# Attention's queries and keys stored in two token orders instead of read with a step

## The chip, the cores and the metric

The kernel runs on one core of a Trainium2 chip. The metric is the device time of one execution in microseconds, as the median of several runs. TensorE multiplies matrices; VectorE, ScalarE and GpSimd work on elements; SyncE issues nearly all transfers, which sixteen DMA engines carry out.

## The reference

One encoder layer runs on 2048 prompt tokens and on 256 sample tokens (2304 in the kernel): RMSNorm and a combined projection; beside each other dilated windowed attention (8 heads of 64) and a bidirectional gated delta rule; then an output projection and a gated feed-forward block. The part that counts here is attention's scores:

```python
DILATED_PATTERNS = ((128, 1), (512, 4), (2048, 16))
...
    def to_sub(t):
        return t.reshape(b, ld, dilation, h, dh).transpose(0, 2, 1, 3, 4).reshape(b * dilation, ld, h, dh)

    num, m, den = _band_attention(to_sub(q), to_sub(k), to_sub(v), window // (2 * dilation))
...
    for part in parts[1:]:
        sc = jnp.exp(part[1] - m_all)
        num = num + part[0] * sc[..., None]
        den = den + part[2] * sc
    return num / den[..., None]
```

Each token attends to 64 neighbours on either side, three times: among all tokens, among those with its residue mod 4, and among those with its residue mod 16. The three results are merged by their denominators. Queries and keys are normalised per head and rotated first.

## The kernel before, in words

**Production** (`att_tile`, line 1341). The normalised input lies in HBM as 9 windows of 256 tokens. A window is loaded (line 240), and for each of its two tiles of 128 tokens and each of two column blocks b (line 1362) TensorE projects queries and keys (`toks`, line 251), VectorE and GpSimd normalise and rotate them, four transposes (line 1393) bring them to channels x tokens, and the result is split into a rounded high part qh (line 1395) and a rest ql (line 1397). Both go to HBM in natural token order (line 1399), in runs of 128 tokens. There are three passes: three windows with both blocks (from line 1417), six windows with block 0 (line 1424), the same six with block 1 (line 1442). The delta rule's scan (`scan`, line 858) takes its steps in between, loading and storing its own operands, and the maxima of head 0 (`first_head`, line 1405) are made in the third pass.

**Attention** (`steady`, line 1227). Heads run one behind the other, 21 groups a head: one for the sample, four of dilation 16, eight pairs of dilation 4, eight of dilation 1. A group has a score step s, an exponential step e (ScalarE, then masks on GpSimd, line 1035) and a value step v. TensorE's order is written out by hand: at step g it issues the scores of group g + 2, some pieces of the next heads' row maxima (line 971, reduced on VectorE at line 974), and the values of group g. Score and maximum products read tokens of one residue as every fourth or sixteenth element of the natural order (`pview`, line 958), both as the weights loaded and as the moving operand:

```python
            nc.tensor.matmul(out, lhsT=kv, rhs=qv, start=True, stop=False)
            nc.tensor.matmul(out, lhsT=k1v, rhs=qlv, start=False, stop=True)
```

The first product contracts over 128 rows: k's high and low parts against q's high part, which VectorE writes twice (`twice_q`, line 945). The second contracts over 65: k's high part with a row of ones (copied by `twice_k`, line 955) against q's low part with a row of negated maxima.

**Loads of a head.** `load_qk` (line 936) and `load_ql` (line 949) bring four tiles of 64 rows x 2304 tokens; q and k have three buffers, the other two tiles two. `load_values` (line 920) brings the values three times, once for each dilation's order, in runs of 64 elements. The maxima go through HBM: `max_store` (line 1008) stores them and loads them back in another order, `max_row` (line 1024) combines them on VectorE, stores the row and loads it into row 64 of ql (line 1032). The denominators take a like way (lines 1189 to 1209). All of this is issued by SyncE into one queue; SyncE's own order is set by a planner from when operands should be ready, while the order on the other four engines in attention is the program's.

## Time and profile before

| | us |
|---|---|
| median of 3 runs (lowest to highest) | 3485.42 (3480.18 to 3487.45) |
| the profiled execution's own time | 3489.7 |
| its span, first to last instruction | 3488.0 |
| TensorE busy | 3300.0 (95%) |
| VectorE busy | 2284.4 (65%) |
| ScalarE busy | 1626.4 (47%) |
| GpSimd busy | 1739.3 (50%) |
| DMA queue of SyncE, share of 16 engines | 46.0% |

Times in the rows count from the span's start. A row of the timeline begins with the start and the duration of what it names; matrix products are pipelined, so the time one product costs is read from start to start, not from its duration. "65*128 65x256" is a product of 65 rows, 128 weight columns and 256 moving columns. "x4" says that four in a row were merged.

### The profile page before, as it was taken

The page shows a single profiled execution, that of the slowest core. Times are in us where ns is not written, and L with a number is a line of the kernel's source. Part 1 is how long each engine was busy: PE and PEld are TensorE (multiplying, and loading weights), DVE is VectorE, ACT ScalarE, POOL GpSimd, SP SyncE. Part 2 cuts the span into 40 slices and gives each one's busy share as a digit, 9 for nine tenths or more (in the row PEclk, how much of TensorE's full clock was granted, in tenths as well). Part 3 has the DMA queues.
Part 4 walks back from the last instruction along what each step waited for, and adds up shares of the span by engine and source line. Part 5 has one row for each costly group of instructions (what it writes and reads, how often), then busy time and mean ns, then how long its engine had stood idle before and what let it go on. Part 6 is the DMA issues. An engine that isn't in the chain of part 4 may idle for free.

```text
span 3488.0 us, 57839 instructions
## 1 busy us (share of the span) xinstructions
PE 3300.0 (95%) x20191; PEld 3005.9 (86%) x20191; DVE 2284.4 (65%) x6044; ACT 1626.4 (47%) x3404; POOL 1739.3 (50%) x1736
## 2 busy tenths in 40 slices
PE   7899899999999979999889899999999999999999
PEld 6888788887987869999677899998899998899998
DVE  7899775675899966675565455557555556555555
ACT  5665534334443346667232444445544445544443
POOL 4323521111345334444122766776866777866774
PEclk9999899999999969999999999999999999999999
DMA  5555555458997865541776422223422222422221
GB/s 186 195 203 202 183 182 171 158 168 280 313 313 217 276 141 111 118 101 46 170 180 150 145 67 66 65 69 97 142 70 61 67 70 79 163 61 67 70 73 49
DMA packets 494313, 483.78 MB, mean 139 GB/s; under 512 B 131303, under 2 KB 405346, under 8 KB 488253
## 3 DMA queue, kind: packets, MB, share of 16 engines
q1 hardware_dynamic: 492357, 474.87, 46.0%
q10 hardware_dynamic: 1296, 4.72, 0.4%
q8 instruction: 160, 2.62, 0.3%
q14 instruction: 132, 1.08, 0.1%
q0 software_dynamic: 368, 0.49, 0.1%
HBM read 337.77 MB, written 142.14 MB: 138 GB/s over the span
## 4 chain that ended last, share of the span: by engine, by line
PE 69%; DVE 17%; DMA 7%; issue 3%; ACT 2%; SPq 1%; POOL 0%; DVEq 0%; ACTq 0%; POOLq 0%
PE psy L1798 5%; PE psy L1799 5%; PE psy L1800 5%; PE psx L1607 4%; PE psx L1606 4%; PE psx L1605 4%; PE pvo L1162 3%; PE psv L1607 3%; PE psv L1605 3%; PE psv L1606 3%; PE pam L971 2%; PE pss L1052 2%; PE pss L1053 2%; PE psh L1322 1%; PE psy L1607 1%
## 5 line engine op out<-in xcount | busy, mean ns | idle before, releaser
L204 POOL TENSOR_TENSOR wring<-ws,wring 128x512 fp32r<-128x512 f32 x260 | 340.1, 1313 | 286.1 <-ACT wring L203 273.0
L1801 DVE TENSOR_TENSOR ya<-ya,psy 128x512 f32<-128x512 f32 x396 | 269.5, 685 | 218.9 <-PE psy L1800 217.4
L1798 PE MATMUL psy<-dh,hh 128*128 128x512 f32 x792 | 311.5, 395 | 7.6 <-ACT hh L1758 6.0
L1799 PE MATMUL psy<-dl,hh 128*128 128x512 f32 x792 | 312.6, 395 | 0.0
L1800 PE MATMUL psy<-dh,hl 128*128 128x512 f32 x792 | 307.5, 396 | 1.5 <-DVE hl L1759 1.5
L203 ACT CAST wring<-ws 128x512 fp32r<-128x512 f32 x260 | 161.3, 620 | 287.1 <-PE psv L1606 143.3
L204 POOL TENSOR_TENSOR wring<-raw,wring 128x512 fp32r<-128x512 f32 x195 | 254.1, 1305 | 72.1 <-ACT wring L203 68.5
L247 PE MATMUL psc<-nt,whi 128*128 128x260 f32 x864 | 255.3, 295 | 27.2 <-DVE kqt L269 5.6
L1035 POOL TENSOR_SCALAR_AFFINE_SELECT pt<-pt 128x256 f32<-128x256 f32 (+3 forms) x400 | 164.7, 435 | 231.1 <-ACT pt L1049 124.9
L249 PE MATMUL psc<-nt,wlo 128*128 128x260 f32 x864 | 251.2, 291 | 0.0
L248 PE MATMUL psc<-nt,whi 128*128 128x260 f32 x864 | 250.6, 290 | 0.0
L203 ACT CAST wring<-raw 128x512 fp32r<-128x512 f32 x195 | 121.0, 621 | 180.9 <-PE psx L1606 93.8
L974 DVE CUSTOM_DVE_ANT_0 mj<-pam,misc 128x256 f32<-128x256 f32 (+2 forms) x400 | 146.6, 367 | 81.0 <-PE pam L971 69.4
L247 PEld LDWEIGHTS psc<-nt,whi 128*128 128x128 f32 x864 | 168.2, 195 | 33.3 <-ACT kqt L261 8.2
L204 POOL TENSOR_TENSOR dl<-raw,dh 128x512 fp32r<-128x512 f32 x132 | 167.5, 1301 | 48.5 <-ACT dh L203 48.5
L1556 POOL TENSOR_TENSOR ws<-raw 128x512 f32<-128x512 f32 x130 | 169.0, 1300 | 24.4 <-DVE hn2l L1514 10.4
L1800 PEld LDWEIGHTS psy<-dh,hl 128*128 128x128 f32 x792 | 148.9, 188 | 35.2 <-DVE hl L1759 2.6
L1798 PEld LDWEIGHTS psy<-dh,hh 128*128 128x128 f32 x792 | 149.0, 188 | 31.2 <-ACT hh L1758 7.3
L249 PEld LDWEIGHTS psc<-nt,wlo 128*128 128x128 f32 x864 | 168.5, 195 | 0.7
L248 PEld LDWEIGHTS psc<-nt,whi 128*128 128x128 f32 x864 | 168.3, 195 | 0.7
L1378 POOL TENSOR_TENSOR r<-xn,ct 128x512 f32<-128x512 f32 x36 | 52.3, 1453 | 229.9 <-DVE xn L1371 189.6
L1799 PEld LDWEIGHTS psy<-dl,hh 128*128 128x128 f32 x792 | 149.2, 188 | 19.0
(435 smaller groups left out, 10615.2 us busy)
## 6 DMA issues: line engine op xcount, KB each, us to landing
raw<-in_w_up SPq DMA_DIRECT2D x260, 256.0 KB
nt<-nt_d SPq DMA_DIRECT2D x20, 2080.0 KB
raw<-in_w_down SPq DMA_DIRECT2D x132, 256.0 KB
nt_d<-nt SPq DMA_DIRECT2D x9, 2080.0 KB
xt<-in_x_prompt SPq DMA_DIRECT2D x24, 512.0 KB
raw<-in_w_in SPq DMA_DIRECT2D x20, 512.0 KB
kq_d<-kqt SPq DMA_DIRECT2D x18, 512.0 KB
kq<-kq_d SPq DMA_DIRECT2D x18, 512.0 KB
```

The costliest lines, as they stand in the source:

```text
L203: nc.scalar.copy(hi, raw)
L204: (sub or nc.gpsimd).tensor_tensor(out=lo, in0=raw, in1=f32(hi), op=ALU.subtract)
L247: nc.tensor.matmul(ps[:, 0:n], lhsT=hi, rhs=f32r(nt[:, 0, k, c0 : c0 + n]), start=k == 0, stop=False)
L248: nc.tensor.matmul(ps[:, 0:n], lhsT=hi, rhs=f32r(nt[:, 1, k, c0 : c0 + n]), start=False, stop=False)
L249: nc.tensor.matmul(ps[:, 0:n], lhsT=lo, rhs=f32r(nt[:, 0, k, c0 : c0 + n]), start=False, stop=k == KT - 1)
L1605: nc.tensor.matmul(ps[:, 0:m], lhsT=hi[:, k], rhs=bh[:, k, 0:m], start=start and k == 0, stop=False, skip_group_check=not start)
L1606: nc.tensor.matmul(ps[:, 0:m], lhsT=hi[:, k], rhs=bl[:, k, 0:m], start=False, stop=False, skip_group_check=not start)
L1607: nc.tensor.matmul(ps[:, 0:m], lhsT=lo[:, k], rhs=bh[:, k, 0:m], start=False, stop=stop and k == KH - 1, skip_group_check=not start)
L1798: nc.tensor.matmul(ps, lhsT=hh, rhs=dh[:, ns], start=gi == 0, stop=False)
L1799: nc.tensor.matmul(ps, lhsT=hh, rhs=dl[:, ns], start=False, stop=False)
L1800: nc.tensor.matmul(ps, lhsT=hl, rhs=dh[:, ns], start=False, stop=gi == len(group) - 1)
L1801: nc.vector.tensor_tensor(out=ya[:, i, ns], in0=ya[:, i, ns], in1=ps, op=ALU.add)
```

## The change

Production also stores queries and keys of the prompt by residue mod 4 (`qr_d`): ScalarE copies each part into an order of four residues, two tiles are gathered, and a window is stored in runs of 64 elements. In the first pass a window's two tiles now run inside the loop over blocks. In attention the first product contracts over 65 rows, high parts with the rows of maxima and ones, in tiles held twice (`firsts`, one set for each parity of the head, each in both orders); the second over 128 rows, k's low part against q's high part and k's high against q's low, in tiles held once and cut into four halves (`seconds`). Dilation 4 now reads contiguous columns, dilation 16 every fourth. The maxima use 64 rows of `firsts`. The order of groups and of the loads in `steady` changes with it.

```diff
     qk_d = [dram.tile([2, 4, P, T], F32, name=f"qk{b}_d") for b in range(2)]
+    qr_d = [dram.tile([2, P, 4, 4, SEQ // 4], F32, name=f"qr{b}_d") for b in range(2)]
...
     sh_d = dram.tile([AH, T], F32, name="sh_d")
+    one_d = dram.tile([1, T], F32, name="one_d")
+    sr_d = dram.tile([AH, SEQ], F32, name="sr_d")
...
-    aorder = [4, 0, 7, 1, 6, 2, 5, 3, 8]
+    aorder = [4, 0, 7, 8, 1, 6, 2, 5, 3]
...
         nc.sync.dma_start(dst[:, 32:48], src[0:SEQ].rearrange("(p r) d -> p r d", r=16))
         yield
         for r in range(4):
             nc.sync.dma_start(
                 dst[:, 16 + 4 * r : 20 + 4 * r], src[0:SEQ].rearrange("(t p r) d -> r p t d", p=P, r=4)[r]
             )
+        yield
         nc.sync.dma_start(dst[:, 0:16], src[0:SEQ].rearrange("(t p) d -> p t d", p=P))
+        nc.sync.dma_start(dst[:, 48:50], src[SEQ:T].rearrange("(t p) d -> p t d", p=P))
...
-    def load_qk(h):
+    HALVES = ((0, 0, 1024), (0, 1024, 2048), (1, 0, 1088), (1, 960, T))
+    def source(h, order, part, key):
         (b, j), rows = divmod(h // 2, 2), head_rows(h)[1]
-        qq, kk = qqs[h % 3], kks[h % 3]
-        nc.sync.dma_start(qq[0:DH], qk_d[b][0, j, rows])
-        nc.sync.dma_start(kk[0:DH], qk_d[b][0, 2 + j, rows])
-        nc.sync.dma_start(kk[DH:P], qk_d[b][1, 2 + j, rows])
-        heads[h].update(qq=qq, kk=kk)
-    def twice_q(h, copy=nc.vector.tensor_copy):
-        qq = heads[h]["qq"]
-        copy(f32r(qq[DH:P]), qq[0:DH])
-    def load_ql(h):
-        (b, j), rows = divmod(h // 2, 2), head_rows(h)[1]
-        heads[h].update(ql=qls[h % 2], k1=k1s[h % 2])
-        return nc.sync.dma_start(qls[h % 2][0:DH], qk_d[b][1, j, rows])
-    def twice_k(h):
-        nc.vector.tensor_copy(f32r(heads[h]["k1"][0:DH]), heads[h]["kk"][0:DH])
-    def pview(ap, dil):
-        return ap[:, 0:SEQ].rearrange("p (n r) -> p r n", r=dil)
+        if order == 0:
+            return qr_d[b][part, rows, 2 * key + j].rearrange("p r m -> p (r m)")
+        return qk_d[b][part, 2 * key + j, rows]
+    def load_first(h, order):
+        n = (SEQ, T)[order]
+        for key in range(2):
+            nc.sync.dma_start(firsts[h % 2][order][key][0:DH, 0:n], source(h, order, 0, key))
+    def load_second(h, half):
+        order, lo, hi = HALVES[half]
+        for key in range(2):
+            for i in range(2):
+                nc.sync.dma_start(seconds[half][key][DH * i : DH * i + DH], source(h, order, i ^ key, key)[:, lo:hi])
+    def load_row(h):
+        nc.sync.dma_start(firsts[h % 2][1][0][DH : DH + 1, 0:T], sh_d[h : h + 1, :])
+        heads[h]["row"] = nc.sync.dma_start(firsts[h % 2][0][0][DH : DH + 1, 0:SEQ], sr_d[h : h + 1, :])
+    def set_ones(h):
+        for order, n in enumerate((SEQ, T)):
+            nc.sync.dma_start(firsts[h % 2][order][1][DH : DH + 1, 0:n], one_d[:, 0:n])
+    def cols(dil, r, lo, hi):
+        if dil == 1:
+            return slice(lo, hi)
+        if dil == 4:
+            return slice(512 * r + lo, 512 * r + hi)
+        return slice(512 * (r % 4) + r // 4 + 4 * lo, 512 * (r % 4) + r // 4 + 4 * (hi - 1) + 1, 4)
...
-        hd = heads[h]
-        q, k = f32r(hd["qq"]), f32r(hd["kk"])
-        mx = hd["mx"] = pe.tile([P, 52], F32, name="mx", bufs=2)
+        mx = heads[h]["mx"] = pe.tile([P, 52], F32, name="mx", bufs=2)
+        q1, k1 = [[f32r(firsts[h % 2][o][key][0:DH]) for o in range(2)] for key in range(2)]
...
+        for r in range(4):
+            piece(
+                [(P * j, P, q1[0][:, cols(16, r + 4 * j, 0, P)], k1[0][:, cols(16, r + 4 * j, 0, P)], band[:, 256:384], 32 + r + 4 * j) for j in range(4)]
+            )
             yield
-        piece([(256 * t, 256, q[:, SEQ + P * t : SEQ + P * t + P], k[:, SEQ:T], scnt[:, t, :], 48 + t) for t in range(2)])
+            for t0 in (0, 2):
+                banded(4, r, t0)
+                yield
+        for t0 in range(0, 16, 2):
+            banded(1, 0, t0)
+            yield
+        piece([(256 * t, 256, q1[1][:, SEQ + P * t : SEQ + P * t + P], k1[1][:, SEQ:T], scnt[:, t, :], 48 + t) for t in range(2)])
         yield
...
-        sh = pe.tile([P, 16], F32R, name="sh", bufs=2)
+        sh = pe.tile([P, 16], F32R, name="sh", bufs=1)
         nc.vector.tensor_scalar(out=sh, in0=mm[:, 0], scalar1=-1.0, scalar2=None, op0=ALU.mult)
+        sr = pe.tile([P, 4, 4], F32R, name="sr", bufs=1)
+        nc.vector.tensor_scalar(
+            out=sr, in0=mm[:, 0].rearrange("p (j r) -> p r j", r=4), scalar1=-1.0, scalar2=None, op0=ALU.mult
+        )
         nc.sync.dma_start(sh_d[h, 0:SEQ].rearrange("(p n) -> p n", n=16), f32(sh))
-        heads[h]["row"] = nc.sync.dma_start(heads[h]["ql"][DH : DH + 1, :], sh_d[h : h + 1, :])
+        nc.sync.dma_start(sr_d[h].rearrange("(r p j) -> p r j", r=4, j=4), f32(sr))
+        load_row(h)
...
-        def score(out, kv, k1v, qv, qlv):
-            nc.tensor.matmul(out, lhsT=kv, rhs=qv, start=True, stop=False)
-            nc.tensor.matmul(out, lhsT=k1v, rhs=qlv, start=False, stop=True)
+        def score(out, half, keys, queries):
+            order, at, _ = HALVES[half]
+            q1, k1 = [f32r(firsts[h % 2][order][key][0 : DH + 1]) for key in range(2)]
+            q2, k2 = [f32r(seconds[half][key]) for key in range(2)]
+            moved = lambda c: slice(c.start - at, c.stop - at, c.step)
+            nc.tensor.matmul(out, lhsT=k1[:, keys], rhs=q1[:, queries], start=True, stop=False)
+            nc.tensor.matmul(out, lhsT=k2[:, moved(keys)], rhs=q2[:, moved(queries)], start=False, stop=True)
...
         def single(r0):
             st = {}
-            kv, k1v, qv, qlv = [pview(x, 16) for x in (kk, k1, qq, ql)]
             def s():
                 ps = st["ps"] = bank("mm", "pss")
                 for u in range(4):
-                    r = r0 + u
-                    score(ps[:, P * u : P * u + P], kv[:, r, :], k1v[:, r, :], qv[:, r, :], qlv[:, r, :])
+                    c = cols(16, r0 + 4 * u, 0, P)
+                    score(ps[:, P * u : P * u + P], r0 // 2, c, c)
...
-                    ks = slice(P * t, P * t + P)
-                    score(ps[:, o : o + hi - lo], kv[:, r, ks], k1v[:, r, ks], qv[:, r, lo:hi], qlv[:, r, lo:hi])
+                    half = 2 + t // 8 if dil == 1 else r // 2
+                    score(ps[:, o : o + hi - lo], half, cols(dil, r, P * t, P * t + P), cols(dil, r, lo, hi))
...
-        out += [single(r0) for r0 in range(0, 16, 4)]
         for r in range(4):
             pts, ob = {}, {}
-            out += [pair(4, 16, r, t0, pts, ob) for t0 in (0, 2)]
+            out += [single(r)] + [pair(4, 16, r, t0, pts, ob) for t0 in (0, 2)]
         pts, ob = {}, {}
         out += [pair(1, 0, 0, t0, pts, ob) for t0 in range(0, 16, 2)]
-        out.insert(0, sample())
+        out.insert(16, sample())
         return out
...
-        direct = {3: (SEQ, T), 15: (0, 448), 17: (448, 960), 19: (960, 1472), 20: (1472, SEQ)}
+        NP1 = 7
+        direct = {14: (0, 448), 16: (448, 960), 17: (SEQ, T), 19: (960, 1472), 20: (1472, SEQ)}
...
-                if (h, g) == (0, 1):
-                    twice_q(1)
-                if (h, g) == (0, GK):
-                    nc.vector.tensor_copy(f32r(k1s[1][DH : DH + 1]), ones[DH : DH + 1, 0:1].to_broadcast([1, T]))
-                if g == 0 and h + 1 < AH:
-                    with tc.issue_after(heads[h]["row"].ins):
-                        ql_in = load_ql(h + 1)
-                    with tc.issue_after((heads[h]["row"] if h else ql_in).ins):
-                        if h + 2 < AH:
-                            load_qk(h + 2)
+                if g == 11 and h + 1 < AH:
+                    with tc.issue_after(tail):
                         for _ in load_values(h + 1):
                             pass
...
                     s, e, _v = todo[n + LAG]
                     s()
                     e()
+                if g == 9 and h + 2 < AH:
+                    load_first(h + 2, 0)
+                if g == 18 and h + 2 < AH:
+                    load_first(h + 2, 1)
+                if g in (3, 9, 13, 18) and h + 1 < AH:
+                    load_second(h + 1, (3, 9, 13, 18).index(g))
                 if h + 1 < AH:
-                    for _ in range(((2 if h == 1 else 1) if g < G1 else 0) if h else (R0 if g >= G0 else 0)):
+                    if (h, g) == (0, 0):
+                        pieces[1] = max_pieces(1)
+                    for _ in range(0 if g > NP1 else 3 if h == 0 and g >= 1 else 2 if g in (3, 5) else g >= 1):
                         next(pieces[h + 1], None)
-                    if g == 1:
-                        twice_k(h + 1)
-                if h + 2 < AH:
-                    g1 = G1 if h else G3
-                    if g == g1 - 2:
-                        twice_q(h + 2)
-                    if g == g1:
+                if h + 2 < AH and g >= NG - 8:
+                    if g == NG - 8:
                         pieces[h + 2] = max_pieces(h + 2)
-                    if g >= g1:
-                        next(pieces[h + 2], None)
+                    for _ in range(1 + g % 2):
+                        next(pieces[h + 2])
                 todo[n][2]()
                 n += 1
                 if h + 1 < AH:
-                    if g == (G1 if h else G2):
+                    if g == NP1:
                         for _ in pieces[h + 1]:
                             pass
                         max_store(h + 1)
-                    if g == (G1 if h else G2) + 4:
+                    if g == NP1 + 4:
                         max_row(h + 1)
                 if h > 0:
                     if g == 4:
                         den_inv(h - 1)
                         den_rows(h - 1, 0)
-                    if g in (9, 13):
-                        den_mul(h - 1, (g - 9) // 4)
-                    if g == 9:
+                    if g in (10, 17 if h < AH - 1 else 13):
+                        den_mul(h - 1, int(g > 10))
+                    if g == 10:
                         den_rows(h - 1, 1)
                 if h == AH - 1 and g in (2, 6, 10, 14):
-                    load_wo(4 + g // 4, staged(pd), *wo[4 + g // 4])
+                    load_wo(4 + g // 4, pd.tile([P, D], F32, name="raw", bufs=1), *wo[4 + g // 4])
...
-        def att_tile(t, nt, c0, blocks):
+        byres = {}
+        def att_tile(t, nt, c0, blocks, last=False):
...
-                rr = rsqrt(pb, ss, [P, AH], 1.0 / DH, EPS, "na")
+                rr = rsqrt(pb, ss, [P, AH], 1.0 / DH, EPS, "na", bufs=1)
...
-                qh = pb.tile([P, 4, P], F32R, name="qh", bufs=2)
+                free = (p3, ("sk", "sq") if t % 2 else ("stk", "su"), 2) if last else (pb, ("qh", "ql"), 1)
+                qh, ql = [free[0].tile([P, 4, P], F32R, name=x, bufs=free[2]) for x in free[1]]
                 nc.scalar.copy(qh, pt.rearrange("p (j t) -> p j t", j=4))
-                ql = pb.tile([P, 4, P], F32R, name="ql", bufs=2)
                 nc.vector.tensor_tensor(out=ql, in0=pt.rearrange("p (j t) -> p j t", j=4), in1=f32(qh), op=ALU.subtract)
                 for i, part in enumerate((qh, ql)):
                     nc.sync.dma_start(
                         qk_d[b][i, :, :, t * P : (t + 1) * P].rearrange("j p t -> p j t"), f32(part)
                     )
+                    if t >= NTP:
+                        continue
+                    if t % 2 == 0:
+                        byres[b, i] = pb.tile([P, 4, 4, 64], F32, name=f"qr{i}", bufs=1)
+                    nc.scalar.copy(
+                        byres[b, i][:, :, :, 32 * (t % 2) : 32 * (t % 2) + 32], f32(part).rearrange("p j (m r) -> p j r m", r=4)
+                    )
+                    if t % 2 == 1:
+                        m0 = 64 * (t // 2)
+                        nc.sync.dma_start(qr_d[b][i, :, :, :, m0 : m0 + 64], byres[b, i])
...
         def first_head():
-            load_qk(0)
-            load_ql(0)
-            nc.scalar.copy(f32r(k1s[0][DH : DH + 1]), ones[DH : DH + 1, 0:1].to_broadcast([1, T]))
-            twice_q(0)
-            twice_k(0)
+            for order in range(2):
+                load_first(0, order)
+            set_ones(0)
...
-            for i in range(2):
+            for b in range(2):
                 with tc.high_priority():
                     scan()
-                att_tile(2 * w + i, nt, 2 + P * i, (0, 1))
+                for i in range(2):
+                    att_tile(2 * w + i, nt, 2 + P * i, (b,))
...
-                for _ in range(FH):
-                    next(fh, None)
-                att_tile(2 * w + i, nts[w], 2 + P * i, (1,))
+                with tc.high_priority():
+                    for _ in range(FH):
+                        next(fh, None)
+                att_tile(2 * w + i, nts[w], 2 + P * i, (1,), wi == NB - 1)
                 scan()
...
+        def second(pool, i):
+            _, lo, hi = HALVES[i]
+            return [pool.tile([P, hi - lo], F32, name=f"{x}2{i}") for x in "qk"]
+        seconds = [second(pa, 0)]
+        load_second(0, 0)
...
+        firsts.append([[pa.tile([DH + 1, n], F32, name=f"{x}1{o}") for x in "qk"] for o, n in enumerate((SEQ, T))])
+        sctx.close()
         pk = kctx.enter_context(pool("at3k"))
-        qqs.append(pk.tile([P, T], F32, name="qq2"))
-        kks.append(pk.tile([P, T], F32, name="kk2"))
-        qls.append(pk.tile([DH + 1, T], F32, name="ql1"))
-        k1s.append(pk.tile([DH + 1, T], F32, name="k1_1"))
-        pieces = {1: max_pieces(1)}
-        sctx.close()
+        seconds += [second(pk, i) for i in range(1, 4)]
+        tail = heads[0]["row"].ins
+        values = load_values(0)
+        for what in (
+            lambda: next(values),
+            lambda: load_first(1, 0),
+            lambda: next(values),
+            lambda: load_second(0, 1),
+            lambda: load_first(1, 1),
+            lambda: set_ones(1),
+            lambda: load_second(0, 2),
+            lambda: list(values),
+            lambda: load_second(0, 3),
+        ):
+            with tc.issue_after(tail):
+                what()
+            tail = nc.cur_bb.bb.instructions[-1]
```

## Rows read from the trace of the kernel before

**Rows 1.** Windows: each engine's busy us, PEclk, DMA share, GB/s, for stretches.
```profile
830.00:955.00 125.00, 124.27 (x874) 114.13 (x873) 95.41 (x305) 55.75 (x166) 30.36 (x29) 1.00 0.98 321
955.00:1130.00 175.00, 160.62 (x919) 137.18 (x918) 163.19 (x529) 71.78 (x225) 84.25 (x85) 0.97 0.83 267
1130.00:1230.00 100.00, 94.42 (x555) 82.72 (x554) 97.49 (x364) 33.63 (x102) 41.98 (x46) 0.98 0.81 255
1317.00:1603.00 286.00, 285.83 (x1875) 284.68 (x1875) 188.43 (x711) 194.20 (x276) 123.99 (x299) 0.99 0.50 103
```

**Rows 2.** Timeline of TensorE: dilation 4, a piece, dilation 1, two more pieces, dilation 16.
```profile
1339.38 0.52 PE L1052 MATMUL pss<-qq,kk 128*128 128x192 f32 x1
...
1340.49 0.85 PE L1162 MATMUL pvo<-pt,va 128*128 128x64 f32 x6
...
1357.16 0.37 PE L971 MATMUL pam<-early,early 128*128 128x256 f32 x2
1357.37 1.08 PE L1162 MATMUL pvo<-pt,va 128*128 128x128 f32 x8
...
1363.95 0.37 PE L1052 MATMUL pss<-qq,kk 128*128 128x256 f32 x1
...
1364.49 0.70 PE L971 MATMUL pam<-early,early 128*128 128x256 f32 x2
1365.01 1.07 PE L1162 MATMUL pvo<-pt,va 128*128 128x128 f32 x8
...
1371.18 0.44 PE L1052 MATMUL pss<-qq,kk 128*128 128x128 f32 x1
...
1373.01 0.77 PE L971 MATMUL pam<-early,early 128*128 128x192 f32 x2
```

**Rows 3.** Lines 947, 956 and 1395: durations in ns, least, median and most.
```profile
L947 DVE CAST qq<-qq x5: 1356/1397/1440, 1264.7 to 1534.7; 64x2304 fp32r<-64x2304 f32 x5
...
L956 DVE CAST k<-kk x3: 1347/1348/1352, 1267.5 to 1570.4; 64x2304 fp32r<-64x2304 f32 x3
...
L1395 ACT CAST qh<-psat x36: 564/586/677, 852.2 to 1249.9; 128x512 fp32r<-128x512 f32 x36
```

**Rows 4.** DMA view of 1370 to 1376, when loads of q and k ran.
```profile
DMA packets 166, 1.24 MB, mean 206 GB/s; under 512 B 32, under 2 KB 32, under 8 KB 32
...
q1 hardware_dynamic: 166, 1.24, 98.1%
```

**Rows 5.** Timeline of TensorE: the sample's first score of heads 1, 6 and 7.
```profile
1316.86 0.36 PE L1052 MATMUL pss<-qq,kk 128*128 128x256 f32 x1
...
1558.71 0.36 PE L1052 MATMUL pss<-early,early 128*128 128x256 f32 x1
...
1603.15 0.36 PE L1052 MATMUL pss<-qq,kk 128*128 128x256 f32 x1
```

**Rows 6.** DMA view of 1317 to 1603: packets, MB and share of SyncE's queue.
```profile
q1 hardware_dynamic: 48316, 29.22, 49.4%
```

**Rows 7.** Timeline of SyncE's issues: the row's first store, its last load, a k load.
```profile
1394.29 0.32 SPq L1018 DMA_DIRECT2D mx_d<-misc  x1
...
1406.83 0.24 SPq L1032 DMA_DIRECT2D ql<-sh_d  x1
...
1414.47 0.59 SPq L941 DMA_DIRECT2D kk<-qk_d  x1
```

**Rows 8.** Timeline of TensorE at attention's start, with its idle time before.
```profile
1270.12 1.62 PE L971 MATMUL pam<-kk,qq 128*128 128x192 f32 x6 [9.05 <-DMA kk<-qk_d]
```

**Rows 9.** DMA view of 1252 to 1257, when values of head 0 were loaded.
```profile
DMA packets 4229, 1.27 MB, mean 254 GB/s; under 512 B 3408, under 2 KB 4229, under 8 KB 4229
...
q1 hardware_dynamic: 4229, 1.27, 120.7%
```

**Rows 10.** DMA view of 1230 to 1236, two stores to qk_d in natural order.
```profile
q1 hardware_dynamic: 1056, 0.52, 29.1%
```

**Rows 11.** DMA view of 1235 to 1320: GB/s in 40 slices of 2.1 us.
```profile
GB/s 0 112 16 93 154 0 36 260 268 254 217 230 243 208 217 217 230 208 208 208 210 202 154 223 239 360 310 32 122 13 0 0 0 8 8 0 4 84 253 245
```

57 lines of the change are left out of this document (25 added, 32 removed).

## The prediction

> **What bounds the kernel now.** I read the stretches first, then one head of attention on TensorE, then the DMA queue. The profiled execution took 3489.7 us (span 3488.0 and 1.7 around it); the median of the runs is 3485.4, so I sum against 3489.7 and take 4.3 off at the end. The change touches two stages: queries and keys are made from about 830 to 1230, in three passes, and attention runs from about 1250 to 1648. The reader should see in [rows 1] that TensorE is busy 285.83 of 286 us in attention while the DMA engines are half busy (0.50). In production it is the other way round: the DMA share is 0.98, 0.83 and 0.81 in the three passes, TensorE is nearly full in the first, and VectorE (97 of 100 us) in the last. So attention can use fewer TensorE microseconds and has DMA time to pay with; production has little of it to give.
>
> Next, what one score costs [rows 2]. A pair group of dilation 4 (192 + 256 columns, keys and queries read at every fourth element) takes 1340.49 - 1339.38 = 1.11 us from its first product to what follows. The same widths read contiguously (dilation 1) take 1364.49 - 1363.95 = 0.54. A maximum piece takes 0.52 at dilation 4 and 0.21 at dilation 1. A group of dilation 16 (every sixteenth element, eight products) takes 1.83.
>
> **What the change takes from TensorE.** Dilation 4 becomes contiguous. Eight pairs a head, 1.11 - 0.54 = 0.57 each: 4.6 us. Eight maximum pieces, 0.52 - 0.21 = 0.31 each: 2.5 us. Together 7.1 us a head. Scores of 8 heads give 36.5, maximum pieces of heads 1 to 7 give 17.4 (head 0's lie in production): 54 us, if nothing else becomes late. Dilation 16 now steps by four elements instead of sixteen. The row nearest to that is dilation 4 of before, which has exactly this step: 1.11 / 4 = 0.28 a product of 224 columns on average, against 1.83 / 8 = 0.23 a product of 128. So a step of four is not cheap, and I take no change. The ends for 48 products a head are +2.4 us (0.28 each) and -4.5 (the contiguous 0.54 / 4 = 0.135 each). The Trainium skill ("SBUF — State Buffer", Door 1) says that a step of up to four fp32 elements is free, since a line has 16 bytes. By that, dilation 4 had nothing to lose, the change would give nothing there, and dilation 16 would gain up to 4.5 us a head. But [rows 2] show twice the price at just that step: the trace disagrees, and the sum stays with the trace. The products keep their number and columns; that they contract over 65 and 128 rows in another order, and the maxima over 64, I cost at nothing. The copies that doubled q and k (1.40 and 1.35 us of VectorE a head, [rows 3]) go; VectorE has 188 of 286 us there, so nothing waits for that.
>
> **What it adds to the DMA queue in attention.** Before, a head loads four tiles of 64 rows x 2304, 0.59 MB each, 2.36 MB. Now: first tiles in two orders, 64 rows x (2048 + 2304) x 2 = 2.23 MB; second tiles in four halves, 1024 + 1024 + 1088 + 1344 = 4480 columns, twice 128 rows, 4.59 MB. Together 6.82 MB, in 20 loads instead of 4. All are loads of 64 rows, and in a stretch that holds almost only such loads the queue moved 206 GB/s at a share of 98% [rows 4]. So 11.5 us a head becomes 33.1, 21.6 more. A head takes 47.7 us now ((1603.15 - 1316.86) / 6, [rows 5]) with the queue busy 49.4% of the time [rows 6], 23.6 us. After: 45.2 us of queue a head, against 47.7 - 7.1 = 40.6 of TensorE. **The queue becomes the bound.** Sixteen more loads, a row and a store are 18 more issues, at the 0.59 us of a load's issue in [rows 7] 11 us of SyncE, which does nothing else.
>
> The queue cannot be full all the time. Loads are released by progress: a half can be overwritten only when its last score is issued, and the first tile for head h+2 is asked for at step 9 and needed at step 13, some 8 us, of which its own transfer is 5.1. The row of maxima goes through four transfers, each waiting for the one before, with VectorE's own turn at step 11 between the second and the third: 1394.29 to 1406.83 = 12.5 us from the first store to the issue of the last load, in a nearly empty queue [rows 7]. From step 7 to step 19, where the next head's first score needs it, are some 24 us. With 5 to 10 us of other loads always ahead, each hop waits; and VectorE, waiting at step 11, holds the maximum pieces and the additions to acc queued behind it, for whose banks TensorE waits. I take 92% use: 45.2 / 0.92 = 49 us a head, against 48.4 for heads 1 to 5 ((1558.71 - 1316.86) / 5, [rows 5]): +3 for five heads. Head 6 has no first tiles to load and keeps some of its gain: -3. Head 7 loads nothing: -4.6, with wo's work around it -4.
>
> Head 0: before, its first scores could start from loaded tiles, and TensorE then waited 9 us for head 1's keys [rows 8]. Now its second half must land before any score, and from about 1250 the queue has 22.3 (second tiles) + 10.8 (head 1's first) + 6.4 (values, 1.64 MB at the 254 GB/s of [rows 9]) = 39.5 us, and within the same head 22.3 + 10.8 + 6.4 for the heads behind: 79 us where the head took 67. Take +8 (ends: 0, since loads for later groups need not land early, and +14). Attention in sum: +3 - 3 - 4 + 8 = +4.
>
> **What it adds in production.** 32 stores of 0.52 MB (2 blocks x 2 parts x 8 windows) in packets of 256 bytes, 2048 each. During the loading of values, 4229 packets, 3408 of them under 512 bytes, went in 5 us [rows 9]; those are loads, but the nearest in size, and give 2.4 us a store. The 512-byte stores of the same tiles took 29.1% of 6 us for 1056 packets [rows 10], 1.65 ns each over all engines, which for 2048 is 3.4 us. I take 2.4: 77 us in all, with 3.4 as the dear end. First pass: 122 busy us of 125, plus 12 stores, 29: 151. Second: 145 + 24 of 175. Third: 81 + 24 of 100. At a share of 1 that is 31 us too much. But the share can pass 1 (120.7% in [rows 9]), which would make room for nearly all of it. I take half: +15. The ends are 0 and +57 (at 3.4 us a store the passes are over by 38, 4 and 15). The 64 new copies on ScalarE, 0.59 us each by the row of qh's own copy [rows 3], 38 us, lie in 400 us of which ScalarE works 161; hidden, and if that cover went they would delay the stores behind them. qh and ql have one buffer instead of two: the next tile waits for the store, and a tile's turn is 400 / 36 = 11 us against stores of 2 to 4; that is free until the queue is backed up, and then it is part of the +15. The tables repeated for a window's second block, and head 0's two copies saved, about cancel on VectorE.
>
> Sum: 3489.7 + 4 + 15 = 3509; less 4.3, about 3505.
>
> **The rivals.** *TensorE stays the bound* (faster). If loads to the two halves of the partitions, which alternate in the second tiles, run beside each other, the seconds cost 11 instead of 22 us and a head's queue time is 34. Then attention gains 54, less 8 for head 0, and with the low price in production (0 to +10) the time is about 3440 to 3450. For it: TensorE is truly full, and the saving is plain in the rows. Against it: at attention's start both halves of kk were loaded one behind the other among six such loads, and once the values are through, the queue stays between 202 and 243 GB/s [rows 11]. The Trainium skill ("SBUF — State Buffer", Can I just issue two DMAs to hit both halves?) says no: two such transfers gained 6%. By that, the second tiles would cost 21 us and the head 44, and my sum stays within 6 us. 0.24.
>
> *The queue binds in the heads, but production hides its stores*: heads at 46 (98% use), -12, head 6 and 7 -7, head 0 +3, production +2: -14, 3471. 0.10.
>
> *The hops and the short leads decide* (slower by much): if the first tile for head h+2 comes 5 us late each time and the row another 2, as with a backlog of one second half (5 us) ahead of each, a head takes 53: +23 for five heads, +14 for head 0, and production at 31: about +60, 3545. It decides from the point where the backlog at step 9 passes 3 us. 0.16.
>
> **How the numbers follow.** The forecast (+8 to +45) has 0.38. Between it and the second rival, within 7 us either way, lie 0.12; 7 us are 0.2%, about what a measurement can tell from no change. So faster 0.34 (the first two rivals), same 0.12, slower 0.54 (forecast and hops). Predicted 3505; range 3448 to 3555, from near TensorE's bound to just past the hops, with some 2 in 10 left out beyond. The forecast's own range is 3492 to 3530.
>
> **What would show it.** Dilation 4 pairs at about 0.55 us and pieces at 0.21; dilation 16 at 1.8. DMA share above 0.9 in heads 1 to 5, rates near 206 to 220 GB/s, and TensorE waiting for second or first tiles or the row at steps 13 and 19. In production a share near or over 1 and TensorE below 120 of 125 in the first pass. Wrong: a head below 44 us, a second-tile rate well above 220 GB/s, or no longer production.

## The result and the profile after

The changed kernel takes **3681.55 us** (median of four runs, 3674.04 to 3688.38) against 3483.94 of before in the same comparison: a ratio of 1.0573 (95% interval 1.0557 to 1.0588), slower. The prediction said 3505, with a range of 3448 to 3555.

To see where 198 us went, one place in the program serves as a mark in every kernel below: the transpose that follows a head's last maximum product (`max_store`, form 128*16), one a head. Between the marks of heads 1 and 7 lie six heads; up to the mark of head 1 lie production and the first part of head 0. Timeline of that line, first before, then after; then the six heads as a window (its length; busy us and number of instructions of TensorE, its weight loads, VectorE, ScalarE and GpSimd; granted clock, DMA share, GB/s):

```profile
L1012 PE MATMUL pmt<-ident,mx x7: 272/272/273, 1303.5 to 1585.8; 128*16 128x128 f32 x7
...
1303.50:1585.80 282.30, 282.30 (x1857) 281.41 (x1857) 191.28 (x739) 190.69 (x269) 119.53 (x290) 0.99 0.50 103
```

```profile
L1040 PE MATMUL pmt<-ident,mx x7: 273/421/421, 1344.5 to 1785.9; 128*16 128x128 f32 x7
...
1344.50:1785.90 441.40, 424.45 (x1897) 386.07 (x1896) 185.36 (x747) 192.76 (x278) 109.03 (x299) 0.59 0.61 134
```

The mark of head 1 comes at 1344.5 instead of 1303.5: **+41** from production and head 0. The window behind it takes 441.4 instead of 282.3: **+159**. What follows the mark of head 7 is 6 us shorter (3682.4 - 1785.9 = 1896.5, before 3488.0 - 1585.8 = 1902.2). This last part varies from 1884 to 1902 us over runs of kernels that have before's code there. Before's own times vary as much (3468 to 3488), but only one of its executions has a trace, so that this is their cause is not shown. I compare kernels by their marks.

One thing has to be allowed for: the kernel before has the mark of head 1 at step 10 of head 0 and all the others at step 7, the changed kernel has every mark at step 7. So before's window is three steps short (1857 products against 1897). Five whole heads, from the mark of head 2 on, first before, then after:

```profile
1345.20:1585.80 240.60, 240.60 (x1581) 239.84 (x1580) 162.14 (x622) 162.80 (x231) 103.17 (x250) 0.99 0.50 103
```

```profile
1419.60:1785.90 366.30, 353.08 (x1582) 321.58 (x1580) 155.84 (x620) 159.93 (x230) 91.69 (x251) 0.59 0.60 133
```

A head takes 73.3 us instead of **48.1**. Before's first interval, 1345.2 - 1303.5 = 41.7, is 6.4 short of that. At equal steps, then, production and head 0 lose about 47 us and six heads about 153. Between kernels with the same marks the windows can be compared as they are.

The window of 441.4 us says what the heads' loss is. TensorE is busy 424 of 441 us with some 1900 products, about as many as before, but its granted clock is **0.59** where it was 0.99. The DMA share is 0.61: the queue, which the prediction made the bound, is not full. Windows of five and of ten microseconds show that 0.59 is a mixture of two levels (same columns):

```profile
1570.00:1575.00 5.00, 5.00 (x45) 4.89 (x43) 3.17 (x4) 4.17 (x8) 2.65 (x9) 1.00 0.70 152
1575.00:1580.00 5.00, 2.28 (x14) 2.07 (x13) 1.07 (x6) 3.15 (x5) 2.47 (x7) 0.99 0.97 204
1580.00:1585.00 5.00, 5.00 (x21) 4.38 (x21) 2.61 (x13) 1.35 (x2) 0.00 (x0) 0.50 1.07 273
...
1595.00:1605.00 10.00, 10.00 (x42) 9.31 (x42) 4.74 (x18) 3.68 (x6) 1.61 (x5) 0.50 0.49 108
1605.00:1615.00 10.00, 10.00 (x45) 9.38 (x44) 3.61 (x18) 3.88 (x6) 2.97 (x8) 0.55 1.03 235
1615.00:1625.00 10.00, 10.00 (x47) 8.93 (x46) 4.53 (x18) 4.38 (x8) 2.97 (x8) 0.62 0.30 68
1625.00:1635.00 10.00, 10.00 (x42) 8.94 (x42) 4.19 (x16) 4.38 (x7) 2.12 (x5) 0.53 0.30 68
1635.00:1645.00 10.00, 9.98 (x78) 9.45 (x77) 4.54 (x14) 7.77 (x12) 4.28 (x12) 1.00 0.39 96
```

The clock is 1.00 (2.4 GHz), falls to 0.50 (1.2 GHz) at 1580, and stays near it for some 50 us in which TensorE is never idle. The timeline shows what TensorE does at the two turns (start, us, line, operation, rows contracted * columns; in brackets idle before and what ended it):

```profile
1565.74 1.65 PE L1197 MATMUL pvo<-pt,va 128*128 128x64 f32 x6
1567.18 0.42 PE L1040 MATMUL pmt<-ident,mx 128*16 128x128 f32 x1
...
1571.41 0.33 PE L1088 MATMUL pss<-q,k 65*128 65x192 f32 x1
...
1571.96 0.83 PE L1197 MATMUL pvo<-pt,va 128*128 128x64 f32 x6
...
1576.13 0.29 PE L1089 MATMUL pss<-q,k 128*128 128x256 f32 x1
1578.96 1.70 PE L987 MATMUL pam<-k,q 64*128 64x128 f32 x6 [2.54 <-DMA k<-qr_d]
```

The full clock returns once the maxima of a head are done (1567.18), and holds through the steps that have none. There a pair of dilation 4 takes 1571.96 - 1571.41 = 0.55 us, against 1.11 in [rows 2]. It goes when the next head's maxima (L987, 64 rows) begin, after a wait of 2.54 us for their tile. So two causes offered themselves: the 64-row products (theory A in the expectations) and the waits for tiles (theory B). Theory C is the forecast's full queue, theory D the second stores.

Production shows, in windows that answer to [rows 1]:

```profile
834.00:960.00 126.00, 124.97 (x843) 113.40 (x843) 107.91 (x330) 69.99 (x164) 38.07 (x44) 1.00 1.00 310
960.00:1135.00 175.00, 153.29 (x941) 134.65 (x939) 139.86 (x502) 98.94 (x293) 72.89 (x72) 0.94 0.99 314
1135.00:1235.00 100.00, 80.99 (x388) 66.29 (x389) 66.75 (x247) 43.78 (x98) 33.53 (x37) 0.85 0.84 245
```

The DMA engines are now full through the first two passes, where they had 0.98 and 0.83, and VectorE's work, 163 us in the second pass before, has slipped.

### The profile page after: what moved, and what is told of

It is laid out like the page before. It is cut to its first block, busy times and chain, and to the rows that moved or that the text cites. A ratio compares the mean times of both kernels' runs of the same rounds, so it can differ in the third digit from the quotient of the medians.

```text
span 3682.4 us, 58209 instructions
## 1 busy us (share of the span) xinstructions
PE 3463.1 (94%) x20191; PEld 3120.7 (85%) x20191; DVE 2256.3 (61%) x6041; ACT 1688.5 (46%) x3467; POOL 1724.6 (47%) x1748
## 3 DMA queue, kind: packets, MB, share of 16 engines
q14 instruction: 135, 1.11, 0.1%
## 4 chain that ended last, share of the span: by engine, by line
PE 73%; DVE 13%; DMA 7%; ACT 2%; issue 2%; POOL 1%; SPq 1%; DVEq 0%; ACTq 0%; POOLq 0%
PE psy L1861 5%; PE psy L1862 5%; PE psy L1863 5%; PE pvo L1197 5%; PE psx L1670 4%; PE psx L1668 4%; PE psx L1669 4%; PE pam L987 3%; PE psv L1670 2%; PE psv L1669 2%; PE psv L1668 2%; PE psh L1355 2%; PE pss L1089 2%; PE psa L259 2%; PE pss L1088 2%
## 5 line engine op out<-in xcount | busy, mean ns | idle before, releaser
L1068 POOL TENSOR_SCALAR_AFFINE_SELECT pt<-pt 128x256 f32<-128x256 f32 (+3 forms) x400 | 149.2, 397 | 407.2 <-ACT pt L1081 327.4
L1080 ACT ACTIVATE pt<-pss,eight 128x512 f32<-128x512 f32 (+1 forms) x168 | 110.4, 657 | 263.8 <-PE pss L1089 262.4
L1197 PE MATMUL pvo<-pt,va 128*128 128x128 f32 (+1 forms) x1024 | 217.5, 379 | 3.8 <-DVE acc L1208 2.1
L1197 PEld LDWEIGHTS pvo<-pt,va 128*128 128x128 f32 x1024 | 193.1, 280 | 21.0 <-issue 14.1
```

What stands on the lines that cost most here:

```text
L1197: nc.tensor.matmul(po[:, o + w0 : o + w1], lhsT=vsel[:, v0 + (t if dil == 1 else 4 * r + t), :], rhs=pts[t][:, off + w0 : off + w1], start ...
```

## The experiments

Runs timed together share their time of before: 3475.1 us for runs 1 to 4, 3468.4 for 5 to 8, 3472.5 for 9 to 12 (median of seven), 3477.1 for 13 and 14. Every other time here is that of one execution, except for run 11 (four). The four executions above differ by 7 us before and by 14 after, so a few microseconds between single times say nothing.

### The rows of the maximum products

**Run 1**: the kernel before, with 64-row maxima and nothing else.

```diff
-        q, k = f32r(hd["qq"]), f32r(hd["kk"])
+        q, k = f32r(hd["qq"][0:DH]), f32r(hd["kk"][0:DH])
```

> The kernel before, whose maximum products contract over 64 rows (high part by high part alone) in place of 128; the small correction of the keys is left out of the maxima. Nothing else is changed: no load, no copy, no order. Theory A (products over 64 rows in the maxima put TensorE on the low clock level, whatever else the heads do): the granted clock in attention falls from 0.98-1.00 to about 0.6, as in the changed kernel, a head goes from 48 to about 65-70 us, and the kernel takes about 3600-3650 us. Theory B (short waits for loads drop the clock and it stays down) and theory C (the DMA queue sets the heads' time): no wait and no transfer is added, so 3484 us within 5, granted clock of attention 0.98 or more.

Measured: 3610.2 us. The six heads as a window:

```profile
1306.00:1713.90 407.90, 407.90 (x1856) 364.24 (x1856) 195.61 (x737) 190.00 (x270) 122.21 (x288) 0.65 0.35 72
```

TensorE is busy for every one of the 407.9 us, so no wait can be the cause, and the DMA share is 0.35. The same number of products takes 126 us more than in the kernel before, at a clock of 0.65. Five whole heads, and two stretches:

```profile
1366.00:1713.90 347.90, 347.90 (x1580) 310.24 (x1578) 166.55 (x622) 161.82 (x231) 106.34 (x250) 0.65 0.34 71
...
1366.00:1396.00 30.00, 30.00 (x183) 26.05 (x181) 19.56 (x68) 17.39 (x27) 11.47 (x30) 1.00 0.51 113
1401.00:1446.00 45.00, 45.00 (x179) 40.38 (x179) 20.61 (x80) 19.79 (x28) 13.28 (x33) 0.50 0.17 34
```

A whole head takes 69.6 us: 21.5 of the 25.1 us a head that the change loses, in the kernel before, by one line. B and C fall as the main cause. The two stretches show more. There is a maximum piece in every step of both, and yet the clock is 1.00 in the first, mostly steps of dilation 1, and 0.50 in the second, mostly steps of dilation 16 and 4. So 64-row products don't hold the low level by themselves; what else in the stream decides it is open. And they are dearer at 1.00 too. From one maximum piece to the next, in steps of the same products, run 1 and then before:

```profile
1374.56 0.50 PE L971 MATMUL pam<-early,early 64*128 64x256 f32 x2
...
1376.34 0.50 PE L971 MATMUL pam<-early,early 64*128 64x256 f32 x2
```

```profile
1400.69 0.40 PE L971 MATMUL pam<-kk,qq 128*128 128x256 f32 x2
...
1402.08 0.40 PE L971 MATMUL pam<-kk,qq 128*128 128x256 f32 x2
```

1.78 us against 1.39: 0.39 for one piece. For the 21 pieces of a head that is by estimate 8 us of the 21.5; the rest goes with the low clock.

**Run 2**: the changed kernel, its maxima over 128 rows of which the upper ones are zero.

```diff
-        q1, k1 = [[f32r(firsts[h % 2][o][key][0:DH]) for o in range(2)] for key in range(2)]
+        q1, k1 = [[f32r(firsts[h % 2][o][key]) for o in range(2)] for key in range(2)]
...
+            nc.gpsimd.memset(x[DH:P], 0.0)
...
+        if h >= 2:
+            nc.sync.dma_start(firsts[h % 2][order][0][DH : DH + 1, 0:n], zero_d[:, 0:n])
```

> The changed kernel, whose maximum products contract over 128 rows again: rows 64 to 127 of its first tiles are set to zero once, and row 64 of the queries is zeroed by two loads of 8 and 9 KB per head ahead of the maxima. Same loads otherwise, same waits, same order, same products' widths. Theory A1 (rows that an instruction contracts over count, whatever they hold): granted clock of attention back to about 1.0, heads of some 43-47 us, attention some 180 us shorter: about 3490-3520 us. Theory A2 (what the rows hold counts, zeros don't help): clock about 0.6, 3680 us. Theory B (waits at step 13 of each head drop the clock): the waits are still there, so clock about 0.6 and 3680 us. Theory C (DMA queue): the queue's work is the same, 3680 us.

Measured: 3542.5 us, 139 less than the changed kernel. The six heads:

```profile
L1043 PE MATMUL pmt<-ident,mx x7: 272/273/278, 1345.6 to 1645.0; 128*16 128x128 f32 x7
...
1345.60:1645.00 299.40, 270.44 (x1896) 266.16 (x1897) 180.58 (x744) 190.22 (x275) 113.99 (x299) 0.93 0.90 193
```

The clock is back at 0.93, though the added rows hold zeros (A1). But the heads take 49.9 us, not the 43 to 47 that I expected: now the DMA share is 0.90 and TensorE is busy only 270 of 299 us. **Run 11** timed this kernel:

> The second run's kernel once more, timed against the kernel before. By the single times, 3542.5 against 3475.1: ratio 1.019, 1.017 to 1.021. By theory A with the production's 46 us and heads of 50 us in place of 47: 42 + 17 - 6 = +53 to +67 us.

3541.5 us (3540.9 to 3545.2), ratio 1.0201 (1.0184 to 1.0218).

**Run 10**: as run 2, but 65 rows.

```diff
-        q1, k1 = [[f32r(firsts[h % 2][o][key]) for o in range(2)] for key in range(2)]
+        q1, k1 = [[f32r(firsts[h % 2][o][key][0 : DH + 1]) for o in range(2)] for key in range(2)]
```

> The second run (zeroed rows), whose maximum products contract over 65 rows in place of 128, row 64 of the queries being zero: one row more than in the changed kernel. If what matters is that a product has 64 rows or fewer: as the second run, heads of 50 us, clock 0.93, 3540 us. If it matters how many rows the products contract over: clock about 0.6 and heads of 73 us, 3680 us. The score's first products have 65 rows and run at the full clock among products of 128 rows, which excludes neither.

3542.1 us, heads of 50.7 us, clock 0.91: one row more than 64 does what 128 do. Its windows around the wait for the next first tile are the counterpart of those above:

```profile
1495.00:1500.00 5.00, 4.84 (x41) 4.55 (x40) 3.20 (x8) 4.87 (x9) 2.89 (x10) 1.00 0.54 118
1500.00:1505.00 5.00, 0.14 (x2) 0.10 (x1) 0.00 (x0) 1.85 (x3) 1.60 (x5) 0.63 0.98 202
1505.00:1510.00 5.00, 5.00 (x23) 5.00 (x24) 2.58 (x13) 0.69 (x1) 0.00 (x0) 0.50 1.06 268
1510.00:1515.00 5.00, 5.00 (x33) 4.97 (x32) 3.14 (x16) 2.52 (x4) 0.77 (x2) 0.84 0.94 221
```

TensorE sits idle for nearly five microseconds, longer than in the changed kernel, and the clock falls too. Then the 65-row maxima run, and the clock is rising again by 1515. So theory B has a part, some microseconds a wait; the 50 us at the low level come only with the 64-row products.

### The queue and the tiles

**Run 3**: the changed kernel without the second tiles' loads after head 0.

```diff
-                if g in (3, 9, 13, 18) and h + 1 < AH:
+                if g in (3, 9, 13, 18) and h + 1 < 0:
```

> The changed kernel without the loads of the second tiles (correction products' operands) for heads 1 to 7; their scores use head 0's second tiles, so the correction of these heads is left out of the computation. 16 of a head's 64-row loads and some 4.5 of its 6.8 MB go away. Theory C (the queue of 64-row loads sets the heads' time, as the prediction had it): heads of some 42-45 us, attention some 180 us shorter, about 3480-3500 us. Theory A (64-row products hold the clock down): the clock stays about 0.6 and the heads about 68 us; only waits of 2 to 3 us per head can go: 3655-3680 us. Theory B (waits for loads drop the clock): the wait for the second tiles goes, that for the first tiles' row may stay; if the clock recovers, 3500-3550 us.

3674.2 us, heads of 72.1 us, clock 0.61, DMA share 0.33. With 64-row maxima the second tiles' loads cost 1.4 us a head: theory C fails for the kernel as it was changed.

**Run 5**: the same edit on run 2.

> The changed kernel with 128-row maximum products (rows 64 to 127 zero, as in the second run) and without the loads of the second tiles for heads 1 to 7, whose scores use head 0's second tiles: the correction of these heads is left out of the computation. If the queue of 64-row loads sets the heads' 49-51 us once the clock is back (step 4 of the prediction), the heads fall to what TensorE needs at the full clock, by the pairs at 0.55 us some 41-44 us, attention is 45-55 us shorter than in the second run and the kernel takes about 3490 us; DMA share about 0.5. If something else sets them (TensorE's own work, ScalarE, GpSimd's selects), heads of 48-50 us and 3535 us.

3522.6 us, heads of 48.0 us: 1.9 a head less than run 2, so the second tiles' loads do cost something there, but with them gone and the queue half empty the heads are no shorter than before's 48.1. What TensorE waits for in the six heads, largest first (us in total, times, longest), in run 2 and then in run 5:

```profile
PE pam L990 <- DMA k<-qr_d: 9.4, 2, 5.2
PE pam L990 <- DMA early<-qr_d: 7.4, 2, 5.1
PE pam L990 <- DMA early<-zero_d: 4.8, 1, 4.8
PE pam L990 <- DMA q<-zero_d: 4.3, 1, 4.3
```

```profile
PE pam L990 <- DMA early<-qr_d: 7.9, 3, 2.7
PE pam L990 <- DMA k<-qr_d: 4.6, 2, 2.6
PE pam L990 <- DMA q<-zero_d: 2.4, 1, 2.4
```

These are the first tiles (`qr_d`, and the zero row loaded with them) for the maxima at step 13, one wait a head: 25.9 us in all in run 2, 14.9 in run 5. The difference, 1.8 a head, is nearly all that the second tiles' loads cost: with them the first tiles come later.

**Run 13**: run 5, without the first tiles' loads either (heads 2 to 7 reuse tiles).

```diff
-                if g == 9 and h + 2 < AH:
+                if g == 9 and h + 2 < 0:
...
-                if g == 18 and h + 2 < AH:
+                if g == 18 and h + 2 < 0:
```

> The fifth run (128-row maximum products with zero rows, no second tiles for heads 1 to 7) without the loads of the first tiles of heads 2 to 7 as well: these heads compute with the tiles of heads 0 and 1, so their scores and maxima are left out of the computation; TensorE's, ScalarE's, VectorE's and GpSimd's instructions are the same. If the waits for the first tiles at step 13, and the low clock that follows each, keep the heads of the fifth run at 48.0 us: clock 0.99 or more, heads of 43-46 us. If the steps without pieces, in which ScalarE is busy 97% and TensorE idles, keep them there: heads of 46.5-48 us, with TensorE busy 90-94% at the full clock.

Run 5, then run 13, over the six heads, and one head of run 13 (TensorE alone):

```profile
1344.10:1632.30 288.20, 269.90 (x1896) 265.76 (x1897) 180.61 (x744) 189.74 (x275) 112.30 (x300) 0.93 0.49 105
```

```profile
1344.80:1609.50 264.70, 261.27 (x1896) 258.20 (x1897) 180.08 (x744) 189.96 (x275) 115.11 (x300) 0.97 0.29 64
...
1432.70:1475.60 42.90, 42.50 (x319) 1.00 0.32 69
```

The single group of dilation 16 in run 13's timeline:

```profile
1452.78 0.47 PE L1091 MATMUL pss<-q,k 65*128 65x128 f32 x1
...
1454.70 1.36 PE L990 MATMUL pam<-early,early 128*128 128x128 f32 x6
```

1454.70 - 1452.78 = 1.92 us with a step of four, against 1.83 with one of sixteen [rows 2]. The kernel takes 3507.4 us; heads of 44.1 us, and 42.9 in a head at the full clock throughout. No wait for a load is left. Nothing was taken from ScalarE, so the steps that it fills do not hold the heads at 48; the waits for the first tiles do, and the low clock after each: 48.0 - 44.1 = 3.9 us a head, 2.5 of them the waits themselves. The six heads of the change can now be read as a sum, for one head: 44.1 without loads, +3.9 for the first tiles, +1.9 for the second, +23.7 for the 64-row products and the low clock that comes with them = 73.6.

**Run 12**: run 2, with the first half of a head's maxima spread.

```diff
-        NP1 = 7
+        NP1 = 9
...
-                    for _ in range(0 if g > NP1 else 3 if h == 0 and g >= 1 else 2 if g in (3, 5) else g >= 1):
+                    for _ in range(0 if g > NP1 else 3 if h == 0 and g >= 1 else g >= 1):
```

> The second run's kernel with the first half of the next head's maximum pieces at one per step in steps 1 to 9, in place of steps 1 to 7 with two in steps 3 and 5. In the fifth run TensorE idled for 1.4 us in each 5 us stretch in which no piece was to be had (ScalarE 97% busy there), so two steps less of that can give 1 to 2 us a head where the queue does not bind: heads of 48-49.5 us, 3530-3540 us. If the queue alone sets the heads: 50 us and 3542 us. If the row comes late for the next head's scores (issued at step 13 in place of 11): heads longer, over 3550 us.

3552.6 us, heads of 52.6 us: a miss. The largest waits of TensorE in it:

```profile
PE pam L990 <- DVE mx L993: 13.4, 6, 4.1
PE pam L990 <- DMA early<-qr_d: 6.0, 2, 3.8
...
PE pss L1091 <- DMA early<-sr_d: 3.9, 3, 2.0
PE pss L1091 <- DMA q<-sr_d: 3.4, 2, 2.6
```

The row (`sr_d`) now came late for the next head's scores, and TensorE waited for a bank that VectorE had not emptied, six times. Run 2 shows neither. This is the cost that the prediction had named for late hops.

**Run 8**: run 2, with the parts laid out in HBM so that one load fills a second tile.

```diff
-            for i in range(2):
-                nc.sync.dma_start(seconds[half][key][DH * i : DH * i + DH], source(h, order, i ^ key, key)[:, lo:hi])
+            nc.sync.dma_start(seconds[half][key], source(h, order, slice(2 * key, 2 * key + 2))[:, :, lo:hi])
```

> The changed kernel with 128-row maximum products (zero rows) and the parts of queries and keys put in HBM so that one load fills all 128 rows of a second tile in place of two loads of 64 rows: as many bytes, half as many of those loads; the stores by residues become 64 of 0.26 MB. If loads that write 128 rows go faster than the 206-215 GB/s that loads of 64 rows show, the queue of a head falls from 49 to about 40 us and the heads go to 42-46 us: about 3500-3520 us. If the rate is the same whatever the rows: heads of 49-51 us and 3540 us, as in the second run.

4115.0 us, heads of 123 us. Busy share of the DMA engines in tenths and GB/s, in 40 slices of 2.5 us, from 1500 to 1600:

```profile
DMA  1111118511111112311111111073891115911112
GB/s 50 52 52 26 39 54 183 91 58 52 54 54 52 51 54 41 56 36 52 52 56 52 54 52 52 22 171 58 208 210 48 59 52 145 234 56 52 52 48 26
```

These loads move 52 GB/s, a quarter of the 206 of [rows 4], with the DMA engines' share at one tenth in most of these slices. My source pattern has an outermost axis of two (high part, low part), and I had not looked at that. The Trainium skill ("DMA: Bandwidth & Descriptors", Rules for kernel authors) says that an outermost axis of fewer than 16 steps confines a transfer to at most as many DMA engines; two busy engines of sixteen would be a share of 0.125, and the share and the rate here agree with that. Whether loads to 128 rows go faster stays open: this run does not tell.

### Production

**Run 4**: the kernel before with the change's copies, second stores, single buffers and order of blocks; it leaves out the change's other order of windows and its earlier turn of head 0's maxima.

```diff
+            for b in range(2):
                 with tc.high_priority():
                     scan()
-                att_tile(2 * w + i, nt, 2 + P * i, (0, 1))
+                for i in range(2):
+                    att_tile(2 * w + i, nt, 2 + P * i, (b,))
...
-                qh = pb.tile([P, 4, P], F32R, name="qh", bufs=2)
+                qh = pb.tile([P, 4, P], F32R, name="qh", bufs=1)
...
+                        nc.sync.dma_start(qr_d[b][i, :, :, :, m0 : m0 + 64], byres[b, i])
```

> The kernel before, with the production part of the change alone: the copies by residues on ScalarE, the 32 stores of 0.52 MB each in 256-byte pieces, the single buffers for the high and low parts, and the two tiles of a window taken block by block; nothing reads the second order. Theory D (these alone make production late by about the 40 us that the changed kernel shows there): about 3520-3530 us, DMA share at or above 0.98 in the first production pass, attention as before (48 us a head). The prediction's step 5: +15 us with ends 0 and +57, about 3500 us. If the lateness in production comes from another part (other window order, first head's pieces ahead of time): 3484-3495 us.

3521.6 us, 46.5 more than before. The mark of head 1 is 48 us late, the window behind it takes 281.6 us as before (282.3): as much as the change loses there at equal steps (47) is in this part alone. **Runs 6 and 7** take it apart: run 6 without copies and stores, run 7 with the copies alone.

> The kernel before, with the two tiles of a window taken block by block and single buffers for the high and low parts: no copies by residues, no second stores. If these two (freedom of order and of buffers) make production late, 3505-3520 us; if the copies or the stores do, 3475-3485 us. My estimate: about 3485 us, since the waits for a buffer come only when the stores are late.

> The same with the copies by residues on ScalarE, without the second stores: what it has over the run without both is the copies, and what the fourth run (3521.6 us) has over it is the stores' 77 us of DMA queue. If the DMA queue makes production late: 3480-3490 us here. If the copies do, through the single buffer that each copy holds longer: 3505-3520 us.

3467.5 and 3471.7 us (before 3468.4): order, single buffers and the 64 copies cost 3 us together, no more than single times differ, and the mark of head 1 comes at 1297.8 and 1301.2 (before 1303.5). The rest is the stores. **Run 9** stores the same bytes in rows of 4 KB.

```diff
-                        m0 = 64 * (t // 2)
-                        nc.sync.dma_start(qr_d[b][i, :, :, :, m0 : m0 + 64], byres[b, i])
+                        w0 = 1024 * (t // 2)
+                        nc.sync.dma_start(
+                            qr_d[b][i].rearrange("p j r m -> p (j r m)")[:, w0 : w0 + 1024], byres[b, i].rearrange("p j r m -> p (j r m)")
+                        )
```

> The fourth run (the kernel before with copies and second stores), whose 32 stores put the same 0.52 MB each in rows of 4 KB one after another in place of pieces of 256 bytes; nothing reads them, so their order is free. If the bytes make production late: 3515-3525 us, as the fourth run. If the pieces of 256 bytes do: 3475-3495 us, next to the 3471.7 us of the run with copies alone. I take the pieces: the prediction's rate for them is 218 GB/s, that of larger ones above 300.

3486.9 us, 14.4 over before. The second pass of runs 7, 4 and 9:

```profile
960.00:1135.00 175.00, 158.80 (x927) 135.41 (x925) 163.70 (x524) 93.03 (x247) 88.41 (x90) 0.99 0.84 271
```

```profile
960.00:1135.00 175.00, 149.85 (x928) 131.40 (x927) 140.02 (x503) 98.19 (x292) 69.60 (x69) 0.95 1.02 320
```

```profile
960.00:1135.00 175.00, 153.07 (x936) 133.15 (x935) 155.09 (x522) 98.87 (x291) 78.41 (x78) 0.96 0.91 306
```

Without the stores the DMA share is 0.84; with them in 256-byte pieces it is 1.02, and VectorE gets through 140 us of work instead of 164; in long rows it is 0.91. By the marks of head 1 (1301.2, 1351.9 and 1317.9 in the same order) the stores cost 51 us, 34 of them for the size of the pieces; by the times, each less its own run of before, 43 and 32.

**Run 14** tried to keep that in a kernel that reads them: run 10, stores in pieces of 1 KB, loads in pieces of 256 bytes.

```diff
-                        nc.sync.dma_start(qr_d[b][i, :, :, :, m0 : m0 + 64], byres[b, i])
+                        nc.sync.dma_start(
+                            qr_d[b][i, :, :, t // 2].rearrange("p j r m -> p j (r m)"), byres[b, i].rearrange("p j r m -> p j (r m)")
+                        )
...
+            for r in range(lo // 512, hi // 512):
+                at = 512 * r - lo
+                nc.sync.dma_start(dst[:, at : at + 512].rearrange("p (w m) -> p w m", w=8), src[:, :, r])
```

> The changed kernel with maximum products over 65 rows and the second order put in HBM by windows: each of the 32 stores in pieces of 1 KB in place of 256 bytes, and the loads of this order, one for each residue, in pieces of 256 bytes. Production by the pieces: +12 to +25 us over before in place of +42 to +48. Loads: if pieces of 256 bytes load at about the 206 GB/s of the long rows to 64 partitions, heads of 50-51 us and 3510-3525 us in all; if at half the rate, the queue of a head grows from 49 to over 65 us and the kernel takes over 3600 us. No theory has it faster than before.

3543.2 us, the same as run 10. Up to head 1's mark it gains 7 us (1333.3 against 1340.3), not the 17 or more that I expected, and the heads take 53.8 us instead of 50.7, at a clock of 0.87: the small pieces moved from the stores to the loads, and a cost with them. Whether that is the pieces' size or the number of loads (24 of this order a head instead of 10) the run does not tell. No kernel that uses the second order is faster than the one before.

## Why the prediction was wrong

- **The step that failed** is the sentence in "What the change takes from TensorE" that costs at nothing "that they contract over 65 and 128 rows in another order, and the maxima over 64". For the part on 65 and 128 rows the runs show no cost. The maxima over 64 rows cost 142 us in the six heads (441.4 against run 2's 299.4), and 140 by the medians (3681.6 - 3541.5; 129 if each is taken less its own runs of before). By run 1 part of that is the products themselves, the larger part the low clock. None of the rivals had it, because all of them took a product's time from its columns and its step, at the clock of before; the granted clock stood in [rows 1] as 0.99 and I never asked what would keep it there. No row that I read shows a 64-row product, so the cost was to be bounded from both sides like the others; a dear end with attention at the lower level, up to as much again as the 286 us of [rows 1], would have held the result.
- **The dilation 4 pair**: right. 0.55 us, as forecast, and its maximum pieces at 0.21 to 0.24 in run 13. Dilation 16, 1.8 us by the forecast, took 1.92: a step of four gains nothing, as [rows 2] had it. The gain of the whole head is smaller than the 7.1 us given: 42.9 us at the full clock without loads, against 47.7, is 4.8. By the timelines about 0.9 of the other 2.3 is dilation 16: four score groups at 1.92 in place of 1.83, and four maximum pieces at about 0.94, by estimate, in place of 0.76 to 0.87. The rest was not traced.
- **The queue as the bound** (49 us a head): wrong for the kernel as it is (share 0.61, run 3). Once the clock is back the figures come out: 49.9 and 50.7 us in runs 2 and 10, share 0.90 and 0.89, where the step said 92% use. The reason holds only in part, so that 49 came so close is partly luck. With the queue at 0.49 a head still takes 48.0 (run 5); what holds it are the waits for first tiles at step 13, which the second tiles' loads lengthen, and without any of these loads TensorE needs 44.1, not 40.6. Second tiles give 1.9 us and first tiles 3.9. The latter were to be felt through waits alone; a part of their cost is the low clock after each wait, which I had not counted.
- **Production, +15 with ends 0 and +57**: mis-sized. The stores alone cost 43 to 51 us (runs 4 and 7), near the dear end. I took 2.4 us a store from loads in 256-byte pieces [rows 9] over the 3.4 us from stores of 512-byte pieces [rows 10], and counted on a share above 1 to make room; it reached 1.02, not 1.2. That 38 us of copies and the single buffers are hidden was right where the queue has room (3 us, runs 6 and 7); what the single buffers cost beside the stores was not separated.
- **Production and head 0 together** were given +23; +41 was measured, +47 at equal steps. With run 2's heads (11 us more than before's in six) the kernel comes to 3541.5 (run 11), inside the range, near the price of the rival "hops and short leads" (3545). Most of that is dear stores. The rival's mechanism is there too: the first tile comes 2.3 to 5.2 us late in each of the six heads of run 2, where it said 5.
- **What would show it** held for the pairs and for production's DMA share (1.00 and 0.99). TensorE below 120 us in the first pass did not show (125.0 of 126); it loses in the second and third. A DMA share near 0.9 showed only with the clock restored. In the six heads TensorE waited at step 13 in the changed kernel and in runs 2, 5 and 10, and for the row only in runs 12 and 14.

## What to carry to other kernels

When a change alters how many rows a product contracts over, look at the granted clock first and compare busy microseconds only at the same clock; here a 65th row of zeros was worth 140 us. Price small-piece stores by stores of the nearest size, where the queue is already full, and remember that turning a layout round moves the small pieces from the store to the load. Before a cheaper engine is counted as a gain, check what then becomes the bound with that engine's work at its new size: here the queue and the short leads took more than all of it: a head of 48.1 us went to 44.1 without loads and to 49.9 with them.
